# Adding the statistics tiles of neighbouring output blocks on GpSimd before TensorE sums them

## The chip, the cores and the metric

The kernel runs on one core of a Trainium2 chip. The metric is the device time of one execution in microseconds; the median of three runs of the kernel before is 2319.44 us (2319.03 to 2321.52).

## The reference, cut to what matters

The reference is a two-layer diffusion trunk over 256 latent tokens and 256 context tokens of 1024 channels. Each layer has three branches: a feed-forward network, a token mixer (latent attention beside a state-space layer), and a second feed-forward network. A branch takes a normed and modulated input and its output is normed, scaled by a gate and added to the residual:

```python
def rmsnorm(x, g):
    xf = x.astype(jnp.float32)
    y = xf * lax.rsqrt(jnp.mean(xf * xf, axis=-1, keepdims=True) + EPS)
    return (y * g.astype(jnp.float32)).astype(x.dtype)

def sublayer_in(h, g_pre, mod, s):
    return rmsnorm(h, g_pre) * (1 + mod[:, 3 * s + 1]) + mod[:, 3 * s]

def sublayer_out(h, y, g_post, mod, s, weight):
    return h + weight * mod[:, 3 * s + 2] * rmsnorm(y, g_post)
```

Between two branches there are thus two norms over the 1024 channels of a token: the one of the branch's output y, and the one of the new residual that the next branch takes in. Both need sums over channels.

## The kernel before, in words

Channels lie on the 128 partitions, in eight blocks of 128; the tokens lie on the columns, 256 of the context (half 0) and 256 latent ones (half 1). So a sum over channels is a sum over partitions, and over the eight blocks. It is made on TensorE: a matmul with a column of ones sums over partitions and adds to what stands in PSUM.

With y the raw output of a branch, G the gate times the norm's weight, and x the residual, the mean square of the new residual follows from three sums: of x², of x·G·y and of (G·y)². The first is carried from branch to branch; the norm of y needs the sum of y² besides. For each output block and half of the tokens `close` (line 765) therefore makes a tile `tri` of 128 x 768 float32 values, three parts of 256 columns: y², (G y)² and x G y. ScalarE makes the squares. The product is made by GpSimd for blocks 0 to 5 and by VectorE for blocks 6 and 7 (the argument `fast`), which are the last of a half. Then `stat` (line 712) adds the tile's column sums to three regions of one PSUM bank, `misc`: four matmuls with a 128 x 32 block of ones, one for each group of 64 tokens, and each goes to its own 32 partitions of the bank. They are plain float32, which the trace shows as two records each, so one tile is eight records of 128x192.

`close` is called for 8 blocks in 2 halves by each of three feed-forward branches and by the first layer's mixer, and for 8 blocks of half 1 alone by the second layer's mixer: 72 tiles. The very last branch doesn't use it. After the last block of a half, `Norm.chain` (line 2036) reads the bank on VectorE, works out both scales in a chain of small instructions (tiles `rs` and `sp`) and spreads them over the partitions with two matmuls; `Norm.block` (line 2065) then makes the next branch's input block by block: VectorE multiplies (`po`), GpSimd adds to the residual `x` (VectorE for the first two blocks), VectorE scales (`pn`), ScalarE and VectorE split into `hhi` and `hlo`, the operands of the next branch's matmuls.

The order of all instructions is made by a list scheduler in the kernel (`Recorder`, lines 220 to 576), with modelled durations: each engine's program is a fixed sequence, issued through the one line 576. A large matmul (128 columns of weights) and a statistics matmul (32 columns) are two modes of TensorE for it. It keeps to one mode while work of that mode is at hand, for up to `TILE_PULL` = 12000 ns of recorded time, or `STAT_PULL` = 1000 ns for the last block's statistics.

On-chip memory is given out in tags: `slot` has 71 buffers of 128x512 (weights as loaded, `raw`, and their two parts `whi` and `wlo`, activations and the rest), `tri` has 4 buffers. A tile takes a buffer at its first write and gives it back after its last use; a load on SP's queue waits for a free slot. Weights stream from HBM throughout, 256 KB a piece; ScalarE and VectorE split each.

Of the kernel before, what the change touches and what calls it, by code (L numbers as in the profile page):

```python
# [13 lines left out]
ALU = mybir.AluOpType  # L14
PSUM = bass.MemoryType.PSUM
DRAM = bass.MemoryType.DRAM
# [6 lines left out]
LEAD = 6  # L23
# [3 lines left out]
SLOTS, HALVES, ROWS, TRIS = 71, 8, 8, 4  # L27
# [9 lines left out]
STAT_PULL = 1000  # L37
LAG = 0
# [34 lines left out]
class View:  # L73
    """A part of an on-chip tile, as strides over [128 partitions, columns]."""
# [55 lines left out]
    def extent(self):  # L130
        """The first partition, the last, and the columns as bits."""
        p, c = divmod(self.offset(), self.root.cols)
        key = c, self.arr.shape[1:], self.arr.strides[1:]
        if key not in MASKS:
            at = np.array([c])
            for n, st in zip(*key[1:]):
                at = (at[:, None] + st * np.arange(n if st else 1)).reshape(-1)
            m = 0
            for x in at.tolist():
                m |= 1 << x  # L140
            MASKS[key] = m
        return p, p + self.arr.shape[0], MASKS[key]
# [14 lines left out]
class Root:  # L157
    """A tile: lasting, or one of a tag's buffers from its first write to its last use."""
# [18 lines left out]
class Scratch:  # L177
    """A part of a DRAM tensor, with what tells it from parts that other instructions use."""
# [41 lines left out]
class Recorder:  # L220
    """Records instructions, then issues them in the order of a list schedule.

    An instruction waits for those that it depends on and for its buffers; each engine takes the one that was
    recorded for the earliest time among those that can run.
    """
# [18 lines left out]
    # ---------------------------------------------------------------- tiles  # L244
# [14 lines left out]
    # ---------------------------------------------------------------- priorities  # L259
    @contextmanager  # L260
    def aside(self, late, pace=0.0, lazy=False):
        """Work beside the main path, as if recorded some time later, and by and by.

        Lazy work is for an engine's idle time, up to the time at which its result is needed.
        """
        old = self.shift, self.side, self.pace, self.lazy
        self.shift, self.side, self.pace, self.lazy = self.shift + late, True, pace, lazy
        yield
        self.shift, self.side, self.pace, self.lazy = old
# [4 lines left out]
    # ---------------------------------------------------------------- recording  # L274
    def cost(self, eng, method, a, kw):
        """Time on the engine, in ns."""
# [101 lines left out]
    # ---------------------------------------------------------------- schedule  # L378
# [166 lines left out]
    def lacks(self, op):  # L545
        """A tile that the instruction is the first to use and that has to wait for a buffer, if there is one.

        A tile gets a buffer only if all that is still to come, in the order of the recording, then fits as well.
        """
        for r in op.roots:  # L550
            if not r.live:
                g = r.tag
                same = sum(not q.live and q.tag is g for q in op.roots)
                if len(g.bufs) < same or r.lo > self.head and (
                        g.held[self.head:r.lo].max() + same > g.size
                        or op.key > self.front + SOON and len(g.bufs) < same + self.SPARE.get(g.name, 0)
                        or op.lazy and op.key > self.front and len(g.bufs) < same + LAZY_SPARE.get(g.name, 0)):
                    return r
        return None
# [19 lines left out]
class Trunk:  # L579
# [24 lines left out]
    # ---------------------------------------------------------------- storage  # L604
# [21 lines left out]
    # ---------------------------------------------------------------- fillers  # L626
    def add_filler(self, gen, interval, delay=0.0, late=0, pace=0.0, lazy=False):
        """A generator whose steps are recorded at intervals, with the priority of a later time.

        With a pace the intervals are that many times VectorE's work in a step.  # L630
        """
        self.fillers.append([self.rec.now + delay, interval, gen, late, pace, lazy])
# [20 lines left out]
    # ---------------------------------------------------------------- weights  # L653
# [8 lines left out]
    def wget(self):  # L662
        """Loads and splits the weights that come next."""
        nc = self.nc
# [13 lines left out]
    # ---------------------------------------------------------------- matmuls  # L678
# [20 lines left out]
    # ---------------------------------------------------------------- norms  # L699
    def part(self, t, h):  # L700
        """Half h of the tokens of a tile: 0 the context, 1 the latent ones, which an x-only tile holds alone."""
# [10 lines left out]
    def stat(self, r, q, n=1):  # L712
        """Adds a block's column sums to n regions of the statistics bank: 4 quadrants by 64 tokens."""
# [5 lines left out]
    def rsqrt(self, v, plain=False, wide=True, times=1.0, mask=None):  # L719
        """times/sqrt of [quadrant, token] rows: as they are, and with the tokens of other quadrants as zeros."""  # L720
# [28 lines left out]
    def rstd(self, r, width, n=1):  # L749
        """1/rms of the sums of squares in n regions from r on."""  # L750
# [4 lines left out]
    def spread(self, p, rows):  # L755
        """Rows of 64 tokens, one of each quadrant, to [128, 256 tokens] on every partition."""
# [8 lines left out]
    def close(self, l, s, i, h, y, src, fast, last=False):  # L765
        """Statistics of half h of block i of a branch's output: sums of src^2, y^2 and x y for y = G src."""
# [16 lines left out]
        self.rec.urgent = False  # L783
        self.rec.pull = None if i < NB - 1 else STAT_PULL
# [3 lines left out]
    # ---------------------------------------------------------------- modulation  # L788
    ADA_AHEAD = 4

    def ada_gen(self, units):
        """One step: one [128, 512] piece of ada_w for the two conditioning vectors."""
# [45 lines left out]
    def ada_first(self):  # L838
        """One step: a quarter of the channels of the two units that the first norm needs."""
# [24 lines left out]
    def ada_rows(self, units):  # L864
        """The same on the vector engine: one step gives 128 channels from their rows of the transposed ada_w."""
# [59 lines left out]
    # ---------------------------------------------------------------- FFN  # L925
    def lead(self, nrm, evac):
        """The first LEAD output blocks of a phase by pairs, one half of the tokens after the other."""
# [29 lines left out]
    def ffn(self, l, f, nrm, nxt):  # L957
        """nrm gives the normed input; nxt(y) makes the Norm that takes the output."""
# [58 lines left out]
    def gate_half(self, g, n):  # L1017
        """Makes the gated block j of half h of the tokens from a bank with both of its products."""
# [7 lines left out]
    def ffn_last(self, l, nrm):  # L1026
        """The last branch: its output has the tokens on partitions, where the norm has one scale per partition."""
# [75 lines left out]
    # ---------------------------------------------------------------- mixer  # L1103
# [197 lines left out]
    def rope(self, t):  # L1301
        """Axial rotation of [128 = two heads of 64, 256 x tokens], in place."""
# [138 lines left out]
    # ---------------------------------------------------------------- S5  # L1441
    def cmul(self, ore, oim, are, aim, bre, bim, tmp):
        """Complex product of equal-shaped views; tmp: two scratch views; outputs may not alias inputs."""
# [8 lines left out]
    def s5_tables(self, l):  # L1452
        """Per-state tables: 192 columns; 0..63 (pair, dir) with (g2, n) on partitions, 64..191 (dir, g) with n twice."""
# [70 lines left out]
        # decay over eight steps  # L1524
# [5 lines left out]
        # unit phases 8, 16, 32, .. steps  # L1530
# [28 lines left out]
        # powers of the transition: 0..7 in the stacked columns, 1..8 in the pair columns  # L1559
# [39 lines left out]
    def s5_build(self, l):  # L1599
        """Per layer: chunk matrices to DRAM. Tensor-engine parts follow their operands by some steps."""  # L1600
# [28 lines left out]
        # rotation tables over the chunks  # L1629
# [16 lines left out]
        for b in range(NB):  # L1646
            stg = self.stg[l][b]
            pa, pb, pc = nxt
            # stacked b_bar in 32-column blocks of a pair, zero elsewhere
# [15 lines left out]
            # readout matrices C a^t and the in-chunk kernels K_t  # L1665
# [40 lines left out]
            # input matrices a^s b_bar, transposed on the tensor engine  # L1706
# [182 lines left out]
    # ---------------------------------------------------------------- program  # L1889
# [38 lines left out]
    def run(self):  # L1928
# [13 lines left out]
        self.have, self.coef, self.gcoef = {}, {}, {}  # L1942
        self.s5t = self.gate = None
# [75 lines left out]
class Norm:  # L2019
    """The end of one branch (its norm and the residual) and the norm that opens the next, by halves of the tokens.  # L2020

    The mean square of the new residual x + G y r follows from the sums of x^2, x G y and (G y)^2.
    """
# [75 lines left out]
# ------------------------------------------------------------------ host layout  # L2099
# [5 lines left out]
def _tok(a):  # L2105
    """[256 tokens, 1024] -> [8 blocks, 128, s, k] with token = 8 k + s."""
    return np.asarray(a).reshape(32, 8, 8, 128).transpose(2, 3, 1, 0)


def _chan(a, axis):  # L2110
    """Channels (block, g, c) -> (block, c, g)."""
# [6 lines left out]
def _blocks(w):  # L2118
    """[K, M] -> [M/128, 128, K/128 * 128]: per output block, K tiles side by side."""
# [93 lines left out]
```

## Time and profile before

| | before |
|---|---|
| median of 3 runs | 2319.44 us |
| span of the profiled execution | 2323.8 us |
| mean granted TensorE clock | 0.991 |
| busy share: TensorE, VectorE, ScalarE, GpSimd | 98%, 80%, 44%, 13% |
| share of the chain that ended last: TensorE | 38% |
| statistics matmuls (`misc<-tri`) | 576 records, 33.0 us busy |

Of the profiled execution the page gives the span alone, and no other time beside it. Busy time of TensorE (PE) is that of matmuls; they are pipelined, so one record's duration overlaps the next one's, and the step from one start to the next tells what an instruction costs. PEld is the loading of weights, DVE is VectorE, ACT ScalarE, POOL GpSimd, SP the engine whose queue issues most of the DMAs (SPq). An arrow `tri<-x,y` is written tile from read tiles.

### The profile page before, as it was taken

How to read it: one execution, taken by the hardware profiler on the slowest of the kernel's cores; microseconds unless marked ns; L12 is line 12 of the kernel's file. 1: busy time of each engine (PE TensorE's matmuls, PEld its weight loads, DVE VectorE, ACT ScalarE, POOL GpSimd, SP SyncE). 2: the span in 40 equal slices, each digit the busy share in tenths (PEclk: the TensorE clock that was granted, in tenths of full speed). 3: DMA queues.
4: the chain of work that ended last, by engine and by line, in shares of the span. 5: the costliest groups of instructions: out<-in, count | busy, mean ns of one | idle time of the engine just before them, and what ended most of it. 6: DMA issues, size and time to landing. Idle time of an engine off the chain costs nothing. (4 is left out here: it accounts for less than half of the span.)

```text
span 2323.8 us, 43733 instructions
## 1 busy us (share of the span) xinstructions
PE 2275.3 (98%) x15768; PEld 1947.8 (84%) x15768; DVE 1870.1 (80%) x4313; ACT 1029.1 (44%) x2050; POOL 300.6 (13%) x455
## 2 busy tenths in 40 slices
PE   8999999999999999999999999999999999998998
PEld 6887878887888888898888888888889898897997
DVE  4997788889889889699997899898557678877554
ACT  5332233653246644543222463333246446575452
POOL 0010111430100200200100131100004110312000
PEclk9999999999999999999999999999999999998999
DMA  9354556966874546243564645656445795673562
GB/s 318 97 162 147 170 186 202 350 194 197 295 256 148 162 147 226 69 123 111 163 197 125 206 148 161 206 191 227 155 137 161 244 299 174 174 258 120 178 195 88
DMA packets 237481, 428.06 MB, mean 184 GB/s; under 512 B 29488, under 2 KB 58032, under 8 KB 237264
## 3 DMA queue, kind: packets, MB, share of 16 engines
q1 hardware_dynamic: 213904, 350.79, 47.8%
q0 software_dynamic: 23360, 74.48, 9.1%
q8 instruction: 124, 2.03, 0.4%
q14 instruction: 93, 0.76, 0.1%
HBM read 366.56 MB, written 58.59 MB: 183 GB/s over the span
## 5 line engine op out<-in xcount | busy, mean ns | idle before, releaser
L576 PE MATMUL acc<-hhi,whi 128*128 128x256 f32 (+2 forms) x2112 | 717.1, 345 | 4.8 <-ACT hhi L576 4.1
L576 PE MATMUL acc<-hhi,wlo 128*128 128x256 f32 (+2 forms) x2112 | 707.6, 343 | 0.0
L576 PE MATMUL acc<-hlo,whi 128*128 128x256 f32 (+2 forms) x2112 | 699.9, 342 | 1.5 <-DVE hlo L576 1.5
L576 ACT ACTIVATE whi<-raw 128x512 fp32r<-128x512 f32 x802 | 476.0, 623 | 367.1 <-PE acc L576 157.8
L576 DVE TENSOR_TENSOR wlo<-raw,whi 128x512 fp32r<-128x512 f32 x802 | 529.6, 686 | 125.4 <-ACT whi L576 75.8
L576 PEld LDWEIGHTS acc<-hhi,whi 128*128 128x128 f32 (+1 forms) x2112 | 398.8, 190 | 56.9 <-ACT hhi L576 6.7
L576 PEld LDWEIGHTS acc<-hhi,wlo 128*128 128x128 f32 (+1 forms) x2112 | 398.9, 190 | 47.5 <-issue 0.6
L576 PEld LDWEIGHTS acc<-hlo,whi 128*128 128x128 f32 (+1 forms) x2112 | 390.3, 189 | 50.8 <-DVE hlo L576 2.8
L576 PE MATMUL acc<-hi,whi 128*128 128x512 f32 (+1 forms) x1144 | 392.4, 345 | 1.5 <-ACT hi L576 1.5
L576 PE MATMUL acc<-lo,whi 128*128 128x512 f32 (+1 forms) x1144 | 389.0, 341 | 0.0
L576 PE MATMUL acc<-hi,wlo 128*128 128x512 f32 (+1 forms) x1144 | 378.8, 343 | 0.6 <-DVE wlo L576 0.6
L576 PEld LDWEIGHTS acc<-hi,whi 128*128 128x128 f32 x1144 | 215.3, 189 | 32.4 <-issue 5.1
L576 PEld LDWEIGHTS acc<-hi,wlo 128*128 128x128 f32 x1144 | 214.3, 189 | 27.6 <-DVE wlo L576 1.8
L576 PEld LDWEIGHTS acc<-lo,whi 128*128 128x128 f32 x1144 | 215.6, 189 | 24.6 <-issue 0.3
L576 ACT ACTIVATE sg<-acc 128x512 f32<-128x512 f32 (+1 forms) x129 | 64.8, 503 | 252.2 <-PE acc L576 234.3
L576 ACT ACTIVATE hi<-sg 128x512 fp32r<-128x512 f32 (+1 forms) x113 | 60.4, 540 | 158.1 <-DVE sg L576 129.6
L576 DVE TENSOR_TENSOR sg<-sg,acc 128x512 f32<-128x512 f32 (+1 forms) x97 | 55.6, 574 | 90.4 <-ACT sg L576 63.4
L576 POOL TENSOR_TENSOR tri<-x,y 128x256 f32<-128x256 f32 x54 | 54.7, 1018 | 323.5 <-ACT y L576 296.1
L576 DVE CUSTOM_DVE_ANT_0 ar<-ar,crow,adab 128x512 f32<-128x512 f32 x104 | 77.6, 750 | 4.5 <-DMA ar<-in_ada_t_dram 4.5
L576 DVE TENSOR_TENSOR lo<-sg,hi 128x512 fp32r<-128x512 f32 (+1 forms) x113 | 66.0, 589 | 17.5 <-ACT hi L576 9.9
L576 DVE CUSTOM_DVE_ANT_0 ar<-ar,crow,ah 128x512 f32<-128x512 f32 x104 | 78.8, 758 | 1.5 <-DMA ar<-in_ada_t_dram 0.9
L576 POOL DMA_DIRECT2D stg<-P x64 | 34.8, 543 | 345.1 <-DVE P L576 345.1
(249 smaller groups left out, 3282.2 us busy)
## 6 DMA issues: line engine op xcount, KB each, us to landing
raw<-in_w_gu_dram SPq DMA_DIRECT2D x352, 256.0 KB, 3.2
ar<-in_ada_t_dram SPq DMA_DIRECT2D x208, 256.0 KB, 3.4
raw<-in_w_dn_dram SPq DMA_DIRECT2D x176, 256.0 KB, 3.2
raw<-in_w_sq_dram SPq DMA_DIRECT2D x128, 256.0 KB, 4.6
raw<-in_w_in_dram SPq DMA_DIRECT2D x112, 256.0 KB, 4.9
m1l<-stg SPq DMA_DIRECT2D x96, 256.0 KB, 5.0
aw<-in_ada_w_dram SPq DMA_DIRECT2D x80, 256.0 KB, 5.8
stg<-P POOLq DMA_DIRECT2D x64, 256.0 KB, 3.8
```

The source lines that it names most:

```text
L576: getattr(getattr(self.tc.nc, engine), method)(*[real(v) for v in a], **{k: real(v) for k, v in kw.items()})
```

## The change: pairs of statistics tiles are added first

`close` now holds back the tile of blocks 0, 2 and 4 of a half. When the tile of block 1, 3 or 5 is made, GpSimd adds the held one to it, all 768 columns in one instruction, and `stat` sums that one tile. Blocks 6 and 7 go to `stat` one by one as before. So a half has five tiles for TensorE in place of eight. A fifth `tri` buffer is added, and `slot` has 69 buffers in place of 71. The rest of the diff takes comments out.

```diff
-SLOTS, HALVES, ROWS, TRIS = 71, 8, 8, 4
+SLOTS, HALVES, ROWS, TRIS = 69, 8, 8, 5
...
 STAT_PULL = 1000
+PAIRED = 6
...
             nc.gpsimd.tensor_tensor(xy, x, y, op=ALU.mult)
         self.rec.urgent = False
+        if i < PAIRED and h in self.held_tri:
+            u = self.held_tri.pop(h)
+            nc.gpsimd.tensor_tensor(t, t, u, op=ALU.add)
+        elif i < PAIRED:
+            self.held_tri[h] = t
+            return
         self.rec.pull = None if i < NB - 1 else STAT_PULL
         self.stat(3 * h, t, 3)
         self.rec.pull = None
...
         self.have, self.coef, self.gcoef = {}, {}, {}
+        self.held_tri = {}
```

## Rows read from the trace of the kernel before

**Rows 1.** The page, part 1: engine, busy us, share of the span, instructions.
```profile
PE 2275.3 (98%) x15768; PEld 1947.8 (84%) x15768; DVE 1870.1 (80%) x4313; ACT 1029.1 (44%) x2050; POOL 300.6 (13%) x455
```

**Rows 2.** TensorE's waits: line waited for, us in total, times, longest.
```profile
PE acc L576 <- DVE sp L576: 6.1, 4, 4.6
...
PE acc L576 <- DVE rs L576: 4.8, 5, 3.3
PE acc L576 <- ACT hhi L576: 4.1, 4, 1.2
...
PE misc L576 <- DVE tri L576: 2.1, 2, 1.4
```

**Rows 3.** Groups of TensorE by shape, the statistics: count, busy us, mean ns.
```profile
L576 PE MATMUL misc<-tri,c 128*32 128x192 f32 x576 | 33.0, 336 | 4.2 <-DVE tri L576 2.1 <-POOL tri L576 1.7 <-ACT tri L576 0.3
```

**Rows 4.** TensorE in order of time, two statistics batches: start us, us, instruction.
```profile
447.59 0.28 PE L576 MATMUL acc<-lo,whi 128*128 128x256 f32 x1
447.71 0.28 PE L576 MATMUL acc<-hi,wlo 128*128 128x256 f32 x1
447.92 1.18 PE L576 MATMUL misc<-tri,c 128*32 128x192 f32 x24
449.04 0.39 PE L576 MATMUL acc<-hi,whi 128*128 128x256 f32 x1
449.26 0.28 PE L576 MATMUL acc<-lo,whi 128*128 128x256 f32 x1
...
449.74 0.28 PE L576 MATMUL acc<-hi,wlo 128*128 128x256 f32 x1
449.95 0.53 PE L576 MATMUL misc<-tri,c 128*32 128x192 f32 x8
450.41 0.39 PE L576 MATMUL acc<-hi,whi 128*128 128x256 f32 x1
```

**Rows 5.** TensorE in order of time, end of the second layer's mixer.
```profile
2109.37 1.18 PE L576 MATMUL misc<-tri,c 128*32 128x192 f32 x24
2110.90 0.53 PE L576 MATMUL misc<-tri,c 128*32 128x192 f32 x8 [0.35 <-ACT tri L576]
2114.78 1.19 PE L576 MATMUL acc<-sp,c 128*128 128x256 f32 x2 [3.35 <-DVE rs L576]
2120.59 1.19 PE L576 MATMUL acc<-sp,c 128*128 128x256 f32 x2 [4.61 <-DVE sp L576]
```

**Rows 6.** GpSimd's groups by shape: count, busy us, mean ns, idle before.
```profile
L576 POOL TENSOR_TENSOR tri<-x,y 128x256 f32<-128x256 f32 x54 | 54.7, 1018 | 323.5 <-ACT y L576 296.1 <-issue 11.8 <-DVE y L576 5.2
...
L576 POOL MEMSET X<- 128x8 f32 x16 | 1.6, 121 | 20.7 <-PE acc L576 17.0 <-DVE X L576 2.4 <-DVE c L576 1.2
```

**Rows 7.** The tile tri: durations in ns, least, median, longest.
```profile
L576 POOL TENSOR_TENSOR tri<-x,y x54: 722/752/6595, 418.9 to 2104.7; 128x256 f32<-128x256 f32 x54
...
L576 DVE SCALAR_TENSOR_TENSOR tri<-x,cG,y x12: 469/479/1048, 444.7 to 1759.2; 128x256 f32<-128x256 f32 x12
```

**Rows 8.** VectorE and GpSimd in order of time, 444 us.
```profile
444.65 1.05 DVE L576 SCALAR_TENSOR_TENSOR tri<-x,cG,y 128x256 f32<-128x256 f32 x1
444.67 0.75 POOL L576 TENSOR_TENSOR tri<-x,y 128x256 f32<-128x256 f32 x1 [0.59 <-DMA m1l<-stg]
```

**Rows 9.** Windows, end of the first branch: length, then PE, PEld, DVE, ACT, POOL busy (x).
```profile
420.00:470.00 50.00, 47.61 (x531) 39.74 (x531) 42.44 (x108) 33.43 (x77) 17.22 (x22) 0.97 0.90 314
```

**Rows 10.** GpSimd in order of time, second half of the first branch.
```profile
455.26 3.14 POOL L576 TENSOR_TENSOR tri<-x,y 128x256 f32<-128x256 f32 x1 [2.59 <-ACT y L576]
459.86 1.60 POOL L576 TENSOR_TENSOR tri<-x,y 128x256 f32<-128x256 f32 x2 [1.47 <-ACT y L576]
461.43 0.72 POOL L576 TENSOR_TENSOR x<-x,po 128x256 f32<-128x256 f32 x1
```

**Rows 11.** The waits of SP's queue, longest in total first.
```profile
SPq L576 <- PE acc L576: 967.8, 486, 19.4
```

**Rows 12.** TensorE in order of time, second layer's mixer, 2006 us.
```profile
2009.93 0.38 PE L576 MATMUL acc<-hi,hi 128*128 128x256 f32 x1 [3.58 <-ACT hi L576]
```

## The prediction

> **What bounds the kernel now.** I read the page first: TensorE's matmuls are busy for 2275.3 of 2323.8 us, 98%, VectorE 80%, GpSimd 13% [rows 1]. TensorE is the bound over the whole length, so an instruction taken off it is worth its step there, unless another engine's work then comes late. I went next to TensorE's waits, to see what comes late already: in a whole execution they are a few us on each releaser, mostly VectorE's norm chains (sp 6.1, rs 4.8) and the operand hhi that follows from them (4.1) [rows 2]. Of the 10.9 us on sp and rs, 3.35 and 4.61 are two waits at one place, the end of the second layer's mixer, where nothing else is left to do while the chain runs [rows 5]. Elsewhere VectorE holds TensorE up very little. Then the groups of TensorE by shape give the statistics: 576 records, 33.0 us busy [rows 3], eight records a tile, so 72 tiles. Busy time is no price here, for the records run beside each other and go at one speed in a batch; the price is read in order of time.
>
> **What is removed.** Two batches with large matmuls on both sides give it [rows 4]. An ordinary step before them is 447.71 - 447.59 = 0.12 us. From the last large matmul before to the first after it is 449.04 - 447.71 = 1.33 us for 24 records and 450.41 - 449.74 = 0.67 for 8. Two tiles more cost 0.66, so a tile costs 0.33 us. What is left of the 0.67 is 0.34; take off the ordinary step of 0.12 and add the slower first step behind a batch, 449.26 - 449.04 = 0.22 in place of 0.12, and a batch as such costs 0.32 us beside its tiles.
>
> Three tiles fewer in each half, in nine halves (four branches with two, the second mixer with one): 27 of 72 tiles, 27 x 0.33 = 8.9 us. Going through the starts of all statistics records, I count 22 batches that stand alone between large matmuls, the first of them that at 447.92 [rows 4], the last that at 2109.37 [rows 5]; the other tiles run among other 32-column matmuls and cost somewhat less, which I put into the bound. With four buffers eight tiles of a half went out in two or more portions; with five buffers and pairs, all five tiles of a half fit at once, and nothing forces a batch in its middle. At best that is 9 batches; I take 13, since at the end of the second halves the last block's tile often comes after the others. That saves 9 x 0.32 = 2.9 us, between 1.3 (18 left) and 4.2 (9 left). The sum on TensorE is 11.8 us, with bounds of 8 and 13.
>
> ScalarE's squares and the products stay. A held tile keeps its buffer some blocks longer; the fifth buffer pays for that, since after three additions three buffers are held, and blocks 6 and 7 take the other two.
>
> **What is added on GpSimd.** 27 additions of 128x768, a width that the trace doesn't show for GpSimd. The least 256-column operation takes 0.72 us [rows 7] and a memset of 8 columns 0.12 [rows 6], so a first estimate is 0.12 + 3 x 0.60 = 1.9 us, at most 3 x 0.75 = 2.25, at least 0.75 if it were all overhead. I take 2.0, being the slope between the two rows that are there: 27 x 2.0 = 54 us on an engine that is idle for 87%. Its own time is not the price; what waits behind it is. Behind it in GpSimd's order stand the residual additions of the next branch's norm: in the first branch x<-x,po at 461.43 runs directly after two products [rows 10], and an addition for blocks 4 and 5 would push it back by up to 2.0 us; the stores of the state-space tables that GpSimd issues wait likewise. The pair's sum on TensorE itself waits for the addition now, but is not late: from block 5 to block 7 of a feed-forward half lie two blocks of 15 large matmuls, 2 x 15 x 0.12 = 3.6 us, longer than the addition, and the norm's chain has to wait for block 7 anyway. The second price is VectorE. At 444.65 its product took 1.05 us beside a GpSimd product of 0.75 that started 0.02 later [rows 8], where 0.48 is its median [rows 7]: it lost 0.57. And GpSimd's operation at 455.26 took 3.14 in place of 0.75 [rows 10]. The two hold each other up, and 2.0 us of GpSimd can hold VectorE up by more than 0.75 can.
>
> How much: at least nothing for an addition that meets no such instruction, at most 2.0 - 0.18 = 1.8 us (the product lost 0.57 of 0.75). I take 1.3, as VectorE also issues instructions that read PSUM and are not held. 27 x 1.3 = 35 us of VectorE, up to 49. In the window with the first branch's statistics VectorE is busy for 42.44 of 50 us [rows 9], so there are 7.6 us of slack for six additions, 7.8 us: it is just filled. Early in a half that costs TensorE nothing, since loaded and split weights lie ahead; late in the last half of a branch, the next branch's operands are awaited. So I charge five additions (blocks 4 and 5, last half of each of the five branches) with 0.7 us each, half of 1.3 as TensorE has some other work: 3.5 us. The bounds are 0 and half of 35, 17 us.
>
> A rule of the Trainium skill says more. In "SBUF — State Buffer", section Who interferes with whom, VectorE instructions with two SBUF inputs and GpSimd instructions that read SBUF exclude each other for the whole of an instruction, and whichever starts first blocks the other fully. The trace agrees (0.57 us lost beside 0.75); by it an addition costs VectorE nearly its whole length, and the third rival below is what follows.
>
> **Slots.** Two buffers of 71 go. The queue of loads waits 967.8 us for buffers that TensorE has yet to free [rows 11], so slots are what lets a load start. A weight piece takes three (raw, whi, wlo), so the look-ahead shortens by two thirds of a piece. In most places data lie far enough ahead. In the second mixer they don't: TensorE stands for 3.58 us before 2009.93 [rows 12]. I take 1.5 us for such places together; below nothing (the order changes, and may fall better) by 1, above at 7, twice that one wait.
>
> **The sum.** -11.8 + 3.5 + 1.5 = -6.8 us on a span of 2323.8, 0.29%. That execution's span is 4.4 us above the median of the runs, which I take as that execution's offset; the change is put on the median: 2319.4 - 6.8 = 2312.6, rounded 2313. About 0.2% (4.6 us) is what a measurement can tell: faster is below 2314.8, slower above 2324.1.
>
> **Rivals.**
> 1. Nothing is given back: VectorE's and GpSimd's delays fall into slack, as nearly all of theirs does today [rows 2]. -11.8 alone gives 2307.6. For it: those waits are small though GpSimd and VectorE hold each other up now. Against: the additions are nearly three times as long.
> 2. Slots: loads come late at several places where today they come just in time. With 7 us for slots and 3.5 on VectorE it is -1.3, thus 2318. For it: the 967.8 us [rows 11]. Against: TensorE's waits name few late weights.
> 3. Slower: in the last half of each branch VectorE is full, and the addition locks it out. At 1.8 us for each of 27 additions it loses 49 us; once more than 11.8 - 1.5 = 10.3 us of that, a fifth, reaches TensorE, the change loses. At 40%, 20 us, it is -11.8 + 20 + 1.5 = +9.7, thus 2329. For it: the 15% of slack in [rows 9] is an average, and in the last third of a branch there is less. Against: TensorE waits only 2.1 us for VectorE's tri today [rows 2], and the statistics can go out at any time in a half.
>
> That fewer tiles are summed can't fail; whether batches merge can, and is in the bounds.
>
> **Chances.** The forecast's case, 2310 to 2318, 0.46, of which 0.38 is below 2314.8; rival 1, below 2310, 0.14; rival 2, 2315 to 2323, 0.20; rival 3, above 2324, 0.20. So faster 0.52, same 0.08 + 0.20 = 0.28, slower 0.20. The range from 2303 to 2326 leaves out the far half of rival 3 and a little below. The likeliest case's own range is 2310 to 2318.
>
> **What would show it.** Right: 360 statistics records; some 13 batches, x40 among them; 27 additions of 1.9 to 2.3 us at their median; TensorE's busy time down by some 10 us; VectorE instructions of twice their length beside the additions. The slot step is wrong if the idle time before that matmul of the second mixer stays at 3.6. Rival 3 is shown by TensorE's waits on sp, rs, hhi and hlo growing by over 10 us in the last halves. The prediction is wrong as a whole if batches stay near 22 or if other stretches, far from the statistics, move by more than 5 us because the order of instructions has changed.

## The result and the profile after

The changed kernel takes 2337.28 us (median of 4 runs, 2335.17 to 2337.8) against 2320.02 us before: a ratio of 1.0069, 95% interval [1.0055, 1.0084]. It is slower by some 16 us, where 2313 had been forecast, with a range to 2326.

The profiled execution after has a span of 2335.0 us. That of before (2323.8) was itself some 4 us above its kernel's median, so the spans differ by less than the medians do; differences between kernels below are taken from the ratios, and the traces serve for the mechanism.

The page, part 1, of the kernel after (busy us, share of the span, instructions) answers to [rows 1]:

```profile
PE 2272.9 (97%) x15552; PEld 1946.5 (83%) x15552; DVE 1908.0 (82%) x4313; ACT 1037.4 (44%) x2050; POOL 353.0 (15%) x482
```

TensorE has 216 records fewer, and is busy for only 2.4 us less. VectorE has exactly as many instructions as before, 4313, and is busy for 37.9 us more. That is the first thing to see: nothing was given to VectorE, and it became slower.

The tile tri in the kernel after (durations in ns, least, median, longest), beside [rows 7]:

```profile
L577 PE MATMUL misc<-tri,c x360: 322/326/529, 427.1 to 2122.0; 128*32 128x192 f32 x180
...
L577 POOL TENSOR_TENSOR tri<-x,y x54: 723/810/5769, 419.5 to 2115.4; 128x256 f32<-128x256 f32 x54
L577 POOL TENSOR_TENSOR tri<-tri,tri x27: 1812/2126/2373, 422.1 to 2116.7; 128x768 f32<-128x768 f32 x27
...
L577 DVE SCALAR_TENSOR_TENSOR tri<-x,cG,y x12: 471/485/1387, 441.5 to 1775.1; 128x256 f32<-128x256 f32 x12
```

The statistics are the 360 records expected, and an addition takes 2.1 us at the median, near the 2.0 estimated. TensorE's waits in the kernel after answer to [rows 2]:

```profile
PE acc L577 <- DVE sp L577: 11.0, 6, 4.6
PE acc L577 <- DVE rs L577: 10.5, 5, 3.8
...
PE acc L577 <- DVE wlo L577: 6.1, 5, 2.1
PE acc L577 <- ACT hhi L577: 5.6, 7, 1.7
PE acc L577 <- DVE hlo L577: 4.3, 5, 3.0
...
PE misc L577 <- POOL tri L577: 0.2, 1, 0.2
```

What grew is nearly all VectorE's: the norm's chain (sp, rs) stands at 21.5 us in place of 10.9, split weights (wlo) at 6.1 where they had been 0.6, hlo at 4.3 where it had been 1.5. Not all of that growth is due to the additions; experiment 1 tells which part. For the added tile itself TensorE waits only 0.2 us, so the pair's sum is not what is late.

One place shows how it happens: the first layer's second feed-forward branch, half 1's blocks running on TensorE while VectorE works out half 0's norm. First GpSimd, then VectorE, then TensorE in the kernel after, in order of time (start us, us, instruction, idle before):

```profile
1349.20 1.84 POOL L577 TENSOR_TENSOR tri<-tri,tri 128x768 f32<-128x768 f32 x1
1351.00 0.74 POOL L577 TENSOR_TENSOR tri<-x,y 128x256 f32<-128x256 f32 x1
...
1355.73 1.81 POOL L577 TENSOR_TENSOR tri<-tri,tri 128x768 f32<-128x768 f32 x1
1357.49 0.74 POOL L577 TENSOR_TENSOR tri<-x,y 128x256 f32<-128x256 f32 x1
```

```profile
1349.68 1.45 DVE L577 TENSOR_TENSOR rs<-rs 128x64 f32<-128x64 f32 x1
1351.05 1.24 DVE L577 TENSOR_TENSOR mt<-mt,mw 128x512 f32<-128x512 f32 x1
...
1355.66 0.41 DVE L577 TENSOR_TENSOR y<-y,acc 128x256 f32<-128x256 f32 x1
1355.99 1.63 DVE L577 SCALAR_TENSOR_TENSOR rs<-rs,rs 128x64 f32<-128x64 f32 x1
1357.55 0.96 DVE L577 SCALAR_TENSOR_TENSOR sp<-rs,sp 128x256 f32<-128x256 f32 x1
```

```profile
1354.55 0.28 PE L577 MATMUL acc<-hi,wlo 128*128 128x256 f32 x1
1358.65 1.19 PE L577 MATMUL acc<-sp,c 128*128 128x256 f32 x2 [3.82 <-DVE rs L577]
...
1363.48 0.41 PE L577 MATMUL acc<-hi,whi 128*128 128x256 f32 x1
1363.70 0.41 PE L577 MATMUL acc<-lo,whi 128*128 128x256 f32 x1
...
1364.11 0.28 PE L577 MATMUL acc<-hi,whi 128*128 128x256 f32 x1
1364.23 0.28 PE L577 MATMUL acc<-lo,whi 128*128 128x256 f32 x1
```

A 64-column instruction of the norm's chain, started at 1349.68 beside an addition, takes 1.45 us, and ends at 1351.13, when GpSimd's addition has ended (1351.04). At 1355.99 it happens again, 1.63 us. The instruction between, y<-y,acc, reads one operand from PSUM and takes its usual 0.41, though the addition had begun before it was done. TensorE's program has the spread (acc<-sp,c) in its fixed place, and stands for 3.82 us. Then its clock: behind the wait large matmuls follow each other by 1363.70 - 1363.48 = 0.22 us, and from 1364.11 on by 0.12 again. In the windows below the granted clock of 1350 to 1370 is 0.86 and 0.80: the lower of the two levels, 1.2 GHz, was granted for part of them, in and behind the idle time, where from 1340 to 1350 it had been the higher one, 2.4 GHz, throughout (1.00). Some twenty matmuls at 0.09 us more are 2 us on top of the 3.82.

Two windows of the kernel after, then one of the kernel before (length; PE, PEld, DVE, ACT, POOL busy; granted clock, DMA share, GB/s):

```profile
1350.00:1360.00 10.00, 6.18 (x45) 5.82 (x44) 10.00 (x22) 5.90 (x13) 5.34 (x5) 0.86 0.44 145
1360.00:1370.00 10.00, 10.00 (x98) 8.92 (x100) 9.50 (x25) 6.14 (x13) 4.42 (x5) 0.80 0.61 192
```

```profile
1350.00:1360.00 10.00, 8.65 (x105) 7.10 (x107) 10.00 (x32) 6.49 (x16) 2.49 (x3) 1.00 0.72 224
```

VectorE is busy for 10.00 of 10 us there, with 22 instructions; the kernel before, at about the same place of the program, had 32 of them in 10.00. It was full already, which an average like that of [rows 9] doesn't show.

### The profile page after: what moved, and what is told of

It is laid out like the page before. It is cut to its first block, busy times and chain, and to the rows that moved or that the text cites. A ratio compares the mean times of both kernels' runs of the same rounds, so it can differ in the third digit from the quotient of the medians.

```text
span 2335.0 us, 43325 instructions
## 1 busy us (share of the span) xinstructions
PE 2272.9 (97%) x15552; PEld 1946.5 (83%) x15552; DVE 1908.0 (82%) x4313; ACT 1037.4 (44%) x2050; POOL 353.0 (15%) x482
## 5 line engine op out<-in xcount | busy, mean ns | idle before, releaser
L577 DVE TENSOR_TENSOR wlo<-raw,whi 128x512 fp32r<-128x512 f32 x802 | 541.9, 703 | 122.9 <-ACT whi L577 74.1
L577 PE MATMUL acc<-hi,wlo 128*128 128x512 f32 (+1 forms) x1144 | 386.0, 345 | 4.0 <-DVE wlo L577 4.0
```

The costliest lines, as they stand in the source:

```text
L577: getattr(getattr(self.tc.nc, engine), method)(*[real(v) for v in a], **{k: real(v) for k, v in kw.items()})
```

## The experiments

The stated theory (A) is that GpSimd's additions lock VectorE out and that this reaches TensorE; the rivals are the two slots fewer (B), another order of instructions or tiles held longer (C), and what is queued behind the addition on GpSimd (D). The list scheduler makes every change of the kernel a change of the whole order. So five experiments keep the order of the changed kernel and alter only what is issued for the 27 additions, in `emit`; all else stands where it stood.

**1. The additions left out, order kept.**

```diff
         for op in self.schedule():
             engine, method, a, kw = op.call
+            if engine == "gpsimd" and method == "tensor_tensor" and a[0].shape[-1] == 768:
+                continue
```

> The changed kernel with its order of instructions kept, but the 27 additions on GpSimd are left out as it is issued (so the tiles of blocks 0, 2 and 4 are missing from the sums). Theory A (the additions lock VectorE out: the changed kernel's VectorE instructions beside GpSimd ones lost some 36 us more than before, and that reached TensorE): about 2309 us, 10 below the kernel before, TensorE's waits on sp, rs, wlo and hlo back at the level of before. Rival B (two slots fewer): stays within 4 us of the changed kernel, 2333 or more. Rival C (another order of instructions, or tiles held longer): stays above 2328.

Measured: 2314.83 us, ratio to before 0.9973 [0.9963, 0.9983]. The same order without the additions is 6.3 us faster than before (10 had been expected), and 22 us faster than with them (1.0069 - 0.9973 = 0.0096 of 2320). B and C fall as causes of the loss: slots and order are still there. A held tile's buffer may come free sooner here; experiments 2 and 3 test that. At the place above, the same spread in this kernel:

```profile
1340.16 0.45 PE L579 MATMUL acc<-sp,c 128*128 128x256 f32 x1 [0.28 <-DVE rs L579]
```

It waits 0.28 us in place of 3.82. Over the whole execution TensorE's waits are:

```profile
PE acc L579 <- DVE sp L579: 7.0, 7, 4.6
...
PE acc L579 <- ACT hhi L579: 5.9, 7, 2.0
PE acc L579 <- DVE hlo L579: 5.7, 7, 4.1
PE acc L579 <- DVE rs L579: 4.3, 4, 3.3
...
PE acc L579 <- DVE wlo L579: 2.2, 1, 2.2
```

The chain (sp, rs) is back at 11.3 us, as it was before, and wlo is down to 2.2. The waits on hlo and hhi are no smaller without the additions, against what was expected: they came with the new order. The page of this kernel gives VectorE's price:

```profile
PE 2263.2 (98%) x15552; PEld 1938.5 (84%) x15552; DVE 1873.2 (81%) x4313; ACT 1033.7 (45%) x2050; POOL 295.9 (13%) x455
```

Same instructions, same order: 1908.0 - 1873.2 = 34.8 us of VectorE are lost to 27 additions, 1.29 us each, and the time grows by 22. In the two profiled executions TensorE stands idle for 62.1 us with the additions (2335.0 - 2272.9) and for 49.0 without (2312.2 - 2263.2), and the same 15552 records are busy for 9.7 us more. So some 13 us of the loss are waits, and some 10 are slower matmuls, at a mean granted clock of 0.987 against 0.992.

**2. A memset in place of each addition, and 3. three memsets.** A memset of the held tile keeps GpSimd occupied and reads nothing from on-chip memory.

```diff
+            if engine == "gpsimd" and method == "tensor_tensor" and a[0].shape[-1] == 768:
+                self.tc.nc.gpsimd.memset(real(a[2]), 0.0)      # three times in experiment 3
+                continue
```

> The changed kernel in its order, each addition replaced by a GpSimd memset of the held tile, 128x768, that writes on-chip memory and reads none (the sums lack the held tiles). Theory A, if only an operation that reads locks VectorE out: within 4 us of the kernel without additions, about 2311. Rival D (what costs is GpSimd's own queue, with the residual additions and stores behind the addition): if the memset takes near 2 us, 2328 or more; at 1 us half of that.

> The changed kernel in its order, each addition replaced by three memsets of the held tile (one took 0.74 us, so GpSimd is occupied for some 2.2 us, as by the addition, but reads nothing; the sums lack the held tiles). Theory A (the lock on what VectorE reads): within 4 us of the kernel without additions, 2311 to 2319. Rival D (GpSimd's queue is what delays): 2328 or more.

Measured: 2316.5 us, 0.9979 [0.9970, 0.9988], with one; 2318.0 us, 0.9983 [0.9974, 0.9992], with three. The groups of GpSimd with three:

```profile
L579 POOL MEMSET tri<- 128x768 f32 x81 | 59.8, 739 | 3.1
L581 POOL TENSOR_TENSOR tri<-x,y 128x256 f32<-128x256 f32 x54 | 51.5, 961 | 289.1 <-ACT y L581 287.7 <-POOL tri L581 0.9
```

Three memsets occupy GpSimd for 59.8 us, more than the additions' 54.6, and the kernel stays 4 us below the one before. VectorE's busy time is 1876.0 us, 2.8 above that without additions. So an occupied GpSimd with all that is queued behind it costs about 2 us (0.0010 of 2320; by the two intervals between nothing and 5), and D falls as the main cause, and with it C's held tiles, for three memsets hold the same tile as long as the addition. What costs is what the memsets lack: the reading.

**4. Each addition in thirds.** Three instructions of 256 columns in place of one of 768, order kept.

```diff
+                for c in range(0, 768, 256):
+                    self.tc.nc.gpsimd.tensor_tensor(*[real(v[:, c:c + 256]) for v in a], **kw)
+                continue
```

> The changed kernel in its order, each addition as three of 128x256 on GpSimd (the same work, three instructions of some 0.75 us). Theory A with the length of one lock as what matters: VectorE gets in between, and some half of the loss comes back, about 2325. Theory A with GpSimd's total time as what matters, and rival D: 2335 or more.

Measured: 2338.37 us, 1.0077 [1.0062, 1.0092], the changed kernel's time within the intervals. The expectation that half would come back was wrong. The thirds in that kernel:

```profile
L579 POOL TENSOR_TENSOR tri<-tri,tri 128x256 f32<-128x256 f32 x81 | 71.7, 912 | 0.0
```

```profile
L579 POOL TENSOR_TENSOR tri<-tri,tri x81: 718/742/1406, 421.8 to 2117.8; 128x256 f32<-128x256 f32 x81
```

VectorE is busy for 1898.8 us, so it did get some of its time back (25.6 us lost in place of 34.8). GpSimd needs 71.7 us in place of 54.6: three instructions of 0.74 us (the median) are 2.2 us already, and the mean of 0.91 shows that some are held up in their turn. TensorE's wait on sp is 12.5 us. Shorter locks didn't end the loss; why the 9 us that VectorE got back bring nothing wasn't separated.

**5. The additions on VectorE, order kept, and 6. scheduled anew.**

```diff
+            if engine == "gpsimd" and method == "tensor_tensor" and a[0].shape[-1] == 768:
+                engine = "vector"
...
-            nc.gpsimd.tensor_tensor(t, t, u, op=ALU.add)
+            nc.vector.tensor_tensor(t, t, u, op=ALU.add)
```

(The first two lines are experiment 5, the last two experiment 6.)

> The changed kernel in its order, the additions issued on VectorE at the same place. Theory A: 27 additions at some 0.87 us are 23 us of VectorE, less than the 36 us that the lock takes; they end sooner, and GpSimd is free. 2322 to 2334, below the changed kernel by 3 us or more. A rival by which VectorE loses less to the lock than the addition costs it: the changed kernel's time or above, 2337 or more.

> The additions on VectorE and the whole scheduled anew, so that the order allows for them. Theory A: most of the 23 us of VectorE finds slack, 2314 to 2326. If VectorE is too full for them wherever they stand: 2328 or more.

Measured: 2326.74 us, 1.0024 [1.0015, 1.0033], with the order kept; 2320.72 us, 0.9998 [0.9988, 1.0008], scheduled anew. The addition on VectorE, order kept:

```profile
L579 DVE TENSOR_TENSOR tri<-tri,tri 128x768 f32<-128x768 f32 x27 | 26.7, 989 | 8.5 <-POOL tri L579 8.4
```

VectorE does the work itself in 0.99 us, where leaving it to GpSimd cost VectorE 1.29. At the same place in the same order it is 0.45% faster on the engine that was to be spared. With the order made for it, it is even with the kernel before: what TensorE saves is given back.

**7. Slots and 8. slots alone.**

```diff
-SLOTS, HALVES, ROWS, TRIS = 69, 8, 8, 5
+SLOTS, HALVES, ROWS, TRIS = 71, 8, 8, 4
```

(On the changed kernel; experiment 8 is the reverse edit on the kernel before.)

> The change with 71 slot buffers and 4 tri buffers as before, scheduled anew. Theory A: 2330 or more, since the additions stay. Rival B (slots): 2322 or less.

> The kernel before with 69 slot buffers and 5 tri buffers, no pairs. Theory A: no cost of its own, 2316 to 2325. Rival B (slots): 2330 or more.

Measured: 2344.98 us, 1.0110 [1.0093, 1.0128], for the change with 71 and 4; 2321.46 us, 1.0000 [0.9991, 1.0009], for the kernel before with 69 and 5. The two slots, with the fifth tri buffer in their place, cost nothing, and the change with four tri buffers and all the slots was worse than with five; whether by the buffer itself or by the order that comes with it wasn't separated. TensorE's wait of 3.58 us in [rows 12] is gone in the changed kernel. It stood before the 125th of the 128 records acc<-hi,hi; the 125th is now the second line below, without a wait, and the first is the 121st, which had waited 0.82 us before:

```profile
2019.45 0.39 PE L577 MATMUL acc<-hi,hi 128*128 128x256 f32 x1 [1.14 <-DVE lo L577]
...
2024.74 0.28 PE L577 MATMUL acc<-hi,hi 128*128 128x256 f32 x1
```

**9 to 11. Fewer pairs, in search of a kernel that beats both.** The condition of the pairing is narrowed, and the whole scheduled anew: to the mixers (`s == 1`) on GpSimd, the same on VectorE, and to the first half (`h == 0`) on GpSimd.

```diff
-        if i < PAIRED and h in self.held_tri:
+        paired = i < PAIRED and s == 1
+        if paired and h in self.held_tri:
```

> Pairs in the two mixers alone (9 additions on GpSimd in place of 27), scheduled anew. Theory A with its price set by VectorE's slack: the mixers, where VectorE is less full, kept nearly what they saved, so 2314 to 2320. If each addition costs the same wherever it stands (22 us over 27, against some 0.3 us of TensorE's that each saves): 2322 to 2328.

> Pairs in the two mixers alone, added on VectorE. Theory A: VectorE's 9 x 0.87 = 8 us find slack there, 2313 to 2320, at or below the one with GpSimd.

> Pairs in the first half of the tokens alone (12 additions on GpSimd, in the four branches that have one), scheduled anew. If the loss comes in the last halves, where the next branch's operands are awaited, as the prediction had it: 2314 to 2322. If it comes in both halves: 2325 or more.

Measured: 2329.38 us, 1.0030 [1.0020, 1.0041]; 2322.87 us, 1.0010 [1.0001, 1.0019]; 2333.68 us, 1.0055 [1.0041, 1.0068]. None beats the kernel before. The hoped-for 2314 to 2320 in the mixers and 2314 to 2322 in the first halves didn't come, and the pairs in the mixers on VectorE came out above their 2313 to 2320. On VectorE it is again cheaper than on GpSimd (by 0.20%, 5 us for 9 additions), in line with experiments 5 and 1. Beyond that they say little, for each has an order of its own: the one with pairs in the mixers falls behind by most at the start of the second layer, some 400 us after the last addition before it. The first halves alone cost 0.55%, which speaks against a loss confined to the last halves, as far as another order lets it. No version run here that makes the whole sums beats the kernel before; experiments 1 to 3, which do beat it, leave part of the sums out.

## Why the prediction was wrong, step by step

The terms of the sum and what they measured (us; measured from the ratios, of 2320):

| step | predicted | measured | from |
|---|---|---|---|
| statistics taken off TensorE | -11.8 | -6.3 (-8.6 to -3.9) | experiment 1, slots and order included |
| additions on GpSimd, through VectorE | +3.5, bounds 0 and 17 | +22 | after against experiment 1 |
| two slots fewer | +1.5 | 0 (-2 to +2) | experiment 8 |
| sum | -6.8 | +16 | after |

**The step that failed** is "I charge five additions (blocks 4 and 5, last half of each of the five branches) with 0.7 us each". VectorE's loss itself was forecast almost exactly: 27 x 1.3 = 35 us, against 34.8. What was wrong is the share that reaches TensorE: a tenth was charged, and the time grew by 22 us, nearly two thirds of 34.8 (about 2 of the 22 may be GpSimd's own queue, by experiment 3), beyond the upper bound of one half. Three things were misread.

First, the slack. The 15% of [rows 9] is the mean of a 50 us window. In windows of 10 us the kernel before shows (columns as above):

```profile
420.00:430.00 10.00, 9.60 (x143) 8.01 (x143) 9.80 (x18) 5.01 (x12) 3.91 (x7) 1.00 1.04 407
430.00:440.00 10.00, 10.00 (x129) 7.92 (x128) 4.60 (x12) 4.01 (x9) 3.06 (x6) 1.00 1.03 363
...
450.00:460.00 10.00, 9.77 (x101) 8.59 (x101) 9.86 (x35) 6.54 (x17) 4.84 (x4) 1.00 0.71 231
460.00:470.00 10.00, 8.25 (x68) 5.94 (x67) 9.93 (x28) 8.39 (x20) 3.19 (x4) 0.83 0.68 190
```

Most of the 7.6 us of idle time lay together, between 430 and 440, where VectorE is busy for 4.60 of 10 us; from 420 to 430 and from 450 to 470 it is full. In the kernel after, the branch's six additions start at 422, 428, 439, 451, 456 and 462 us: all but one come in full stretches.

Second, where the time goes in. The norm's chain of half 0 runs on VectorE while half 1's blocks close. So the additions of half 1's earlier blocks, not only those of blocks 4 and 5, meet the chain, as at 1349.68 and 1355.99; and VectorE's program is a fixed sequence, so all behind a blocked instruction is late with it. Beside the wait of 3.82 us, these stand before spreads of half 0 in the kernel after:

```profile
454.84 0.67 PE L577 MATMUL acc<-sp,c 128*128 128x256 f32 x2 [2.39 <-DVE rs L577]
...
974.53 0.78 PE L577 MATMUL acc<-sp,c 128*128 128x256 f32 x2 [1.94 <-DVE sp L577]
...
1770.09 1.02 PE L577 MATMUL acc<-sp,c 128*128 128x256 f32 x2 [3.38 <-DVE sp L577]
```

In experiment 1 the same four spreads wait 0.19, 0.29, 0.28 and 0.89 us: 9.9 us less in all, most of the 13 us of waits. The second mixer, which has no half 0, shows no such wait; there the chain is awaited as long without the additions as with them.

Third, small waits today were taken as a sign of slack. [Rows 2] showed that VectorE's present losses, 0.57 us where one of its instructions is hit [rows 8], hardly reach TensorE. An addition costs 1.29 us on the mean, and the waits didn't stay small: sp and rs stand at 21.5 us with the additions and at 11.3 without them, in the same order. Behind such a wait the granted clock is lower too, and matmuls follow each other by 0.21 us in place of 0.12 for some 5 us, a cost that the prediction had no term for: of the 22 us some 10, as the busy times in experiment 1 show.

The rule of the Trainium skill that the prediction weighed ("SBUF — State Buffer", section Who interferes with whom) held in each point that the runs tried: an instruction on VectorE with two on-chip inputs is blocked to the end of GpSimd's (1.45 us beside 1.84), one that reads PSUM for one of its two inputs is not (0.41 at 1772.14, wholly within an addition), and GpSimd instructions that only write cost VectorE next to nothing (experiments 2 and 3). Which of two goes first [rows 8] doesn't show: VectorE's product began 0.02 us ahead and was the one to lose. And an instruction of VectorE with one input was held too: at 450.96, beside an addition of 1.83 us from 450.70, it took 1.63 us where 0.19 is its median without the additions. GpSimd, then VectorE in the kernel after:

```profile
1771.74 2.15 POOL L577 TENSOR_TENSOR tri<-tri,tri 128x768 f32<-128x768 f32 x1
```

```profile
450.96 1.63 DVE L577 TENSOR_SCALAR rs<-rs 128x64 f32<-128x64 f32 x1
...
1772.14 0.41 DVE L577 TENSOR_TENSOR y<-y,acc 128x256 f32<-128x256 f32 x1
```

The lock was given a rival with 0.20 of the chance. That rival had its mechanism and sign right, and it had said that the slack of [rows 9] is an average; it put the point from which it decides at a fifth of VectorE's loss, and two thirds came through. Its sign came as well: the waits on sp, rs, hhi and hlo grew from 16.5 to 31.4 us, though 22.9 are there without the additions.

**Statistics.** Removal is smaller than forecast. 27 tiles at 0.33 us stand as counted, 8.9 us, but the batches hardly merged: 18 stand alone where 22 did and 13 were taken, the first at 444.45 and the last at 2120.40 (two more, at 462.21 and 466.60, have 32-column matmuls right behind them). The largest is one of four tiles, and at the end of the mixer the last tile still goes alone:

```profile
957.27 1.51 PE L577 MATMUL misc<-tri,c 128*32 128x192 f32 x32
...
2120.40 0.86 PE L577 MATMUL misc<-tri,c 128*32 128x192 f32 x16
2121.83 0.53 PE L577 MATMUL misc<-tri,c 128*32 128x192 f32 x8 [0.57 <-ACT tri L577]
```

So 2.9 us for batches became 4 x 0.32 = 1.3, and the rows support some 10.2 us; 6.3 arrive in experiment 1, and its interval reaches to 8.6. Another order of instructions is in that number too. From the spread at 1850.30 to the one at 2114.78 [rows 5], the second mixer of the kernel before, are 264.5 us; between the same two in experiment 1 are 257.0:

```profile
1850.30 0.59 PE L576 MATMUL acc<-sp,c 128*128 128x256 f32 x2
```

```profile
1845.82 0.59 PE L579 MATMUL acc<-sp,c 128*128 128x256 f32 x2
...
2102.79 1.19 PE L579 MATMUL acc<-sp,c 128*128 128x256 f32 x2 [3.35 <-DVE rs L579]
```

These 7.5 us are most of the 11.6 by which the two profiled executions differ, where three tiles fewer are worth 1 us. So the sign that other stretches move by more than 5 us with the order came true, and how the 6.3 us divide between statistics and order stays open.

**Slots** were charged 1.5 us and cost nothing in experiment 8. The wait that was to tell, 3.58 us [rows 12], neither stayed nor grew; it is gone. That the queue's 967.8 us [rows 11] are waits for buffers needed only later, and so no delay, would explain it; no run here shows it.

## What to carry to other kernels

Moving work from a full engine to an idle one is free only if the idle one, at work, holds up no third: GpSimd stood idle for 87% of the time, yet each us of its additions took 0.64 us (34.8 of 54.6) from VectorE, which was the second busiest. Price such a move as work on the engine that it locks, at the place where it stands, and read that engine's slack there in windows of a few us rather than over a stage. Where the locked engine does the same work in less time than the lock costs it, give it the work, or leave the change undone: here the additions on VectorE came out even with the kernel before (0.9998), not ahead.

## What the runs showed of the hardware that had not been expected

Cutting a GpSimd addition into thirds leaves the kernel's time as it was (1.0077 against 1.0069): VectorE recovers 9 us, and GpSimd's additions grow from 54.6 to 71.7 us in all. A GpSimd memset of 128x768 takes 0.74 us and an addition 2.02 us on the mean; the memsets, at 59.8 us in all, cost VectorE 2.8 us, and the additions 34.8.
